# Four accumulator banks a group, the chained bank seeded by ScalarE, in a float32 decoder-layer kernel

## The chip, the cores and the metric

The kernel runs on one core of a Trainium2 chip. The metric is the device time of one execution in microseconds (us). The engines are TensorE (PE in the profile, its weight loads PEld), VectorE (DVE), ScalarE (ACT), GpSimd (POOL) and SyncE (SP, which issues most of the loads). Each has its own instruction queue, worked off in order.

## The reference, cut to what matters

One decoder layer on 256 tokens of width 2048, all in float32, with some 350 MB of weights by their shapes:

```python
h = rmsnorm(x, g_mix);  proj = h @ w_in            # 2048 -> 15872
x_r, g_r, q, k, v, gate_r, gate_a = split(proj)
y_r = (gelu(g_r) * rg_lru(conv(x_r))) @ w_rnn_out  # 2816 -> 2048
y_a = stick_breaking_attention(norm(q), norm(k), v) @ w_attn_out
x = x + (sigmoid(gate_r) * y_r + sigmoid(gate_a) * y_a) @ w_o
g, u = split(rmsnorm(x, g_ffn) @ w_ffn_gu)         # 2048 -> 2 * 5632
x = x + (silu(g) * u) @ w_ffn_down                 # 5632 -> 2048
x = x + sigmoid(rmsnorm(x, g_ple) @ w_ple_gate) * (p @ w_ple_proj)
```

Nearly all of the work is in these matrix products.

## The kernel before, in words

**Products.** Every float32 operand is split in two rounded halves (`hi` from ScalarE, `lo = x - hi` from VectorE). One product of a 128x128 token tile with a 128x512 block of weights is then three matmuls, `hi*hi`, `hi*lo`, `lo*hi` (`prod`). The splits of weights are the tiles `whi`/`wlo` (plain chunks, from `raw`) and `shi`/`slo` (chunks of the seven-product scheme, from `r`), each 128x1024; a chunk is loaded by one DMA of 512 KB.

**Groups.** `group` computes four output banks, two token tiles by two column blocks of 512 (`cols[0]`, `cols[1]`). A k tile is 128 rows of the weights. For some pairs of k tiles (listed in `CFG`) the 2x2x2 block product is done with seven products in place of eight (Winograd's form of Strassen's scheme); the pairs come in twos, a double pair (`dp`), since a chunk holds 1024 columns. The seven steps are named `11`, `22`, `21` (weight blocks as loaded) and `T1` to `T4` (sums of weight blocks, made in place in the tile `r`: by a DMA that adds, issued by POOL (`pr.add`), where the step is listed in `how`, else by VectorE, `r<-r,r`). All other k tiles are plain: each chunk, one k tile of both column blocks, feeds four products.

**Banks before.** A group takes five of the eight PSUM banks: the outputs `q2`, `q4`, `q3`, `q8`, and `U`, in which `11`, `T1`, `T2`, `T3` are accumulated one after the other. At the stations between, `U` is read: ScalarE copies it after `11` (`ja`), VectorE subtracts after `T1` (`je = ja - U`), ScalarE copies it after `T2` (`jc`) and after `T3` (`jd`), and VectorE adds `je = jd + je`. At the end VectorE joins each of the four output banks with one of these four (`join`, or `onto` where the result is added to the residual `x1`).

**Order.** `build` records every operation with its tiles in program order. `schedule` then plans each engine's order with a table of costs, due times counted back from the PE order, and numbers of slots (`ROOM`: 42 tiles of 4 KB, 22 of 2 KB, 8 banks); PE may take an operation up to `WINDOW` = 60 places ahead. `emit` writes the instructions in the planned order, once, so on the chip every queue follows that order whatever happens.

**Stages**, in PE's order before: `xr` (five groups and a half), `ro`, `gtr`, `v`, `qk` with attention between, `gta`, `ao`, `wo`, then `gu` and `dn` mixed, then `pg` with `pp`.

Of the kernel before, what the change touches and what calls it, by code (L numbers as in the profile page):

```python
# [36 lines left out]
class Tile:  # L37


    def __init__(self, name, kind, cols, dt=F32):  # L40
        self.name, self.kind, self.cols, self.dt = name, kind, cols, dt
        self.log, self.ops, self.real, self.slot, self.n = [], [], None, None, 0
# [45 lines left out]
class Program:  # L88
# [102 lines left out]
    def mms(self, jobs, reads, writes, name=""):  # L191


        jobs = list(jobs)
        d = sum(j[3] for j in jobs)

        def emit(nc):
            for o, l, r, _, start, stop in jobs:
                nc.tensor.matmul(o.ap(), l.ap(), r.ap(), start=start, stop=stop)
        return self.op("PE", d, 0.2, emit, reads, writes, name=name)  # L200

    def prod(self, ps, x, w, name=""):
# [5 lines left out]
        def emit(nc, start, stop, again):  # L208
            kw = {"skip_group_check": True} if again else {}
            nc.tensor.matmul(ps.ap(), x[0].ap(), w[0].ap(), start=start, stop=False, **kw)  # L210
            nc.tensor.matmul(ps.ap(), x[0].ap(), w[1].ap(), start=False, stop=False, **kw)  # L211
            nc.tensor.matmul(ps.ap(), x[1].ap(), w[0].ap(), start=False, stop=stop, **kw)  # L212
# [3 lines left out]
    def turns(self, ps, srcs, ident, name=""):  # L216


        def emit(nc):
            for n, s in enumerate(srcs):  # L220
                nc.tensor.transpose(ps[n * P:n * P + P].ap(), s.ap(), ident.ap())  # L221
        return self.op("PE", 0.109 * len(srcs), 0.25, emit, [*srcs, ident], [ps[:P * len(srcs)]], name=name)
# [15 lines left out]
LOAD_US, ADD_US, DMA_LEAD, DMA_TAIL, SPARE, LATE = 1.575 / 512, 2.96 / 512, 1.3, 1.2, 5.0, 2.0  # L238
# [6 lines left out]
def deadlines(prog, boost=None):  # L245
# [5 lines left out]
    for o in reversed(prog.ops):  # L251
# [3 lines left out]
        fin = o.at + (40.0 if o.cap is None else o.cap)  # L255
# [11 lines left out]
def schedule(prog, room, window, boost=None):  # L267
# [15 lines left out]
    free = {k: [(0.0, i, None) for i in range(n)] for k, n in room.items()}  # L283
    pes = [o for o in prog.ops if o.eng == "PE"]
# [13 lines left out]
    def can(o):  # L298
# [4 lines left out]
        for k, ts in want.items():  # L303
            m = max((t.need, t.n) for t in ts)
            i = bisect.bisect_left(wait[k], m)
            if len(free[k]) <= i:
                return False
# [7 lines left out]
    while left or events:  # L315
        moved = True
        while moved:
            moved = False
            for e in ready:
# [11 lines left out]
                else:  # L331
                    for i, (k, _, o) in enumerate(ready[e]):
                        if best is not None and k > best + 3.0:
                            break
                        if o.early is not None and now < o.due - o.early:
# [19 lines left out]
                for t in o.tiles:  # L355
                    if t.kind in room and t.slot is None:
                        if o.eng == "SP":
                            i = max(range(len(free[t.kind])), key=lambda i: free[t.kind][i][:2])
                        else:
                            i = 0  # L360
                        _, t.slot, o.why = free[t.kind].pop(i)
# [23 lines left out]
                moved = True  # L385
        if not events:
            if left:
                for e in ready:
                    print(e, [(round(k, 1), o.name, can(o)) for k, _, o in ready[e][:5]])
                print({k: len(v) for k, v in free.items()},  # L390
                      {k: [(t.name, round(t.need)) for _, _, t in v[:6]] for k, v in wait.items()})
                raise RuntimeError(f"no room at {now}")
            break
        now = events[0][0]
        while events and events[0][0] <= now + 1e-9:
# [7 lines left out]
            for t in o.tiles:  # L403
                t.left -= 1
                if t.left == 0 and t.kind in room:
                    bisect.insort(free[t.kind], (now, t.slot, o), key=lambda x: x[:2])
# [36 lines left out]
def emit(prog, order, nc, tc, pools):  # L443
    first, last, opened = {}, {}, {}
    again, shut = set(), set()
    for o in order:
        for r in o.reads:
            if r.t.kind == "P":
                for k in [k for k in opened if k[0] is r.t and overlap(k[1], k[2], r.a, r.b)]:
                    last[opened.pop(k).n] = True  # L450
                    shut.add(k)
        for r in o.acc:
            k = (r.t, r.a, r.b)
            if k not in first:
                first[k] = o
            if k in shut:
                again.add(o.n)
# [5 lines left out]
    for o in order:  # L463
        for t in o.tiles:
            if t.real is None and t.kind in pools:
                pool = pools[t.kind]
                names[t.name] = names.get(t.name, 0) + 1
                tag = f"{t.kind}{t.slot}" if t.slot is not None else f"k_{t.name}"
# [5 lines left out]
        if o.acc:  # L474
            r = o.acc[0]
            k = (r.t, r.a, r.b)
            o.emit(nc, first[k] is o, o.n in last, o.n in again)
# [14 lines left out]
SPREAD = (0.3, 0.5, 0.65, 0.8)  # L492


def order_of(ks, nd, lead=0):


    ks = list(ks)
    if not nd:
        return ks  # L500
    if lead:
        return ks[:lead] + order_of(ks[lead:], nd)
    n = len(ks)
    cuts = [round(n * f) for f in SPREAD]
    p = [ks[i:j] for i, j in zip([0] + cuts, cuts + [n])]
    s = {m: [(m, d) for d in range(nd)] for m in ("11", "22", "T1", "21", "T2", "T3", "T4")}
    h = (nd + 1) // 2
    return (s["11"] + s["22"] + p[0] + s["T1"] + s["21"][:h] + p[1] + s["T2"] + s["21"][h:] + p[2] + s["T3"] + p[3]
            + s["T4"] + p[4])


def build(cfg):
# [31 lines left out]
    for n in ("h", "l"):  # L544
# [5 lines left out]
    warm = tile("warm", "P")  # L550
    pr.mms([(warm.all, ones_r.all, w1t[0].all, 0.4, True, True) for _ in range(9)], [ones_r.all, w1t[0].all], [warm.all],
           name="warm")
# [64 lines left out]
    def half_sums(h, name):  # L617
# [5 lines left out]
        tt(s1, a22, a21, ALU.subtract, name="hs")  # L623
        stt(s2, s1, -1.0, a11, ALU.mult, ALU.subtract, name="hs")
# [28 lines left out]
    def group(w, cols, ks, pairs, sums, tokens, how, hooks=None, lead=0):  # L653
# [6 lines left out]
        q2, q4, q3, q8 = (psum("q") for _ in range(4))  # L660
        U = psum("u") if nd else None
        chain = {}
        a = e = c = d = None
# [5 lines left out]
        bank = {"21": q2, "22": q3, "T4": q4}  # L669
        for n, x in enumerate(order):  # L670
# [9 lines left out]
            m, dp = x  # L680
            if m in ("11", "22", "21"):
                r, b = {"11": (0, 0), "21": (1, 0), "22": (1, 1)}[m]
                chain[m, dp], chain["b" + m, dp] = raw_of(src(r, b, dp), "r" + m)
# [746 lines left out]
```

## Time and profile before

| | |
|---|---|
| median of the runs shown (3) | 1820.9 us (1820.66 to 1825.76) |
| the profiled execution | 1822.8 us, of which the span from first to last instruction is 1821.1 us |
| PE busy | 1797.6 us, 99% of the span, 8325 matmuls |
| VectorE busy | 1742.5 us, 96%, 2076 instructions |
| ScalarE busy | 1351.9 us, 74%, 1803 instructions |
| POOL busy | 176.3 us, 10%; 200 adding DMAs of 512 KB |
| mean share of the 16 DMA engines | 81%; 420 MB moved |
| mean granted TensorE clock | 0.997 |

A busy PE in this profile is not a PE at its peak: a matmul row lasts 390 ns, yet the next one starts 227 ns later. How much PE loses is read from the distances between starts, not from the busy share.

### The profile page before, as it was taken

The numbers are of one execution on the slowest core, as the hardware profiler recorded it, in microseconds if no ns is written. First come the engines' busy times: TensorE is split into PE (matmuls) and PEld (weight loads), VectorE is DVE, ScalarE is ACT, GpSimd is POOL, SyncE is SP. The second block draws the span as 40 slices with busy tenths as digits, with TensorE's granted clock in tenths as the row PEclk, the third lists the DMA queues.
The fourth block names the chain that finished last, engine by engine and source line by source line (L and its number), as shares of the span: only waits on it lengthen the run. The fifth ranks groups of instructions, "written<-read, shape, count | busy, mean of one in ns | idle before, by whom it ended". The sixth has DMA issues, their size and how long they took to land. (4 is left out here: it accounts for less than half of the span.)

```text
span 1821.1 us, 24029 instructions
## 1 busy us (share of the span) xinstructions
PE 1797.6 (99%) x8325; PEld 1489.7 (82%) x8325; DVE 1742.5 (96%) x2076; ACT 1351.9 (74%) x1803; POOL 176.3 (10%) x209
## 2 busy tenths in 40 slices
PE   9899999999999999999999999999999999999998
PEld 7788888788887888888878888778888788888887
DVE  8999997989999889999899999999999999999998
ACT  7889999856766687889666876666677666767774
POOL 1000000001110110010110011100111001110000
PEclk9999999999999999999999999999999999999999
DMA  9676676689997987768987788788988789889684
GB/s 356 197 213 201 194 211 199 195 245 266 249 251 226 244 238 207 212 188 237 267 251 244 235 229 221 214 227 247 285 238 233 195 246 266 226 236 278 197 233 131
DMA packets 118490, 420.09 MB, mean 231 GB/s; under 512 B 13280, under 2 KB 13664, under 8 KB 118368
## 3 DMA queue, kind: packets, MB, share of 16 engines
q1 hardware_dynamic: 89424, 313.68, 49.0%
q0 software_dynamic: 28800, 104.87, 31.6%
q8 instruction: 65, 1.06, 0.2%
q14 instruction: 57, 0.47, 0.1%
q10 hardware_dynamic: 144, 0.01, 0.0%
HBM read 416.41 MB, written 2.10 MB: 230 GB/s over the span
## 5 line engine op out<-in xcount | busy, mean ns | idle before, releaser
L175 ACT ACTIVATE shi<-r 128x1024 fp32r<-128x1024 f32 x644 | 659.2, 1053 | 233.5 <-DVE r L142 93.2
L142 DVE TENSOR_TENSOR slo<-r,shi 128x1024 fp32r<-128x1024 f32 x644 | 774.4, 1239 | 22.5 <-ACT shi L175 20.8
L142 DVE TENSOR_TENSOR wlo<-raw,whi 128x1024 fp32r<-128x1024 f32 (+2 forms) x310 | 375.5, 1219 | 17.2 <-ACT whi L175 11.1
L175 ACT ACTIVATE whi<-raw 128x1024 fp32r<-128x1024 f32 (+2 forms) x310 | 318.9, 1040 | 49.6 <-PE q L211 15.5
L188 POOL DMA_DIRECT2D r<-in_w_dram x200 | 174.3, 872 | 1605.6 <-DVE slo L142 528.3
L142 DVE TENSOR_TENSOR r<-r,r 128x1024 f32<-128x1024 f32 x168 | 206.6, 1242 | 0.3
L211 PE MATMUL q<-wlo,xg 128*128 128x512 f32 x464 | 182.0, 392 | 2.2 <-DVE wlo L142 1.9
L210 PE MATMUL q<-whi,xg 128*128 128x512 f32 x464 | 182.7, 394 | 0.7 <-ACT whi L175 0.7
L212 PE MATMUL q<-whi,xg 128*128 128x512 f32 x464 | 181.1, 390 | 0.0
L211 PEld LDWEIGHTS q<-wlo,xg 128*128 128x128 f32 x464 | 87.2, 188 | 23.0 <-DVE wlo L142 6.1
L212 PEld LDWEIGHTS q<-whi,xg 128*128 128x128 f32 x464 | 87.1, 188 | 18.5 <-DVE xg L146 0.4
L210 PEld LDWEIGHTS q<-whi,xg 128*128 128x128 f32 x464 | 87.2, 188 | 18.3 <-ACT whi L175 1.1
L211 PE MATMUL u<-slo,hgs 128*128 128x512 f32 x192 | 75.8, 395 | 2.9 <-DVE slo L142 2.9
L211 PE MATMUL u<-slo,xs 128*128 128x512 f32 x198 | 77.9, 394 | 0.6 <-DVE slo L142 0.6
L210 PE MATMUL u<-shi,xs 128*128 128x512 f32 x198 | 78.1, 395 | 0.0
L212 PE MATMUL u<-shi,xs 128*128 128x512 f32 x198 | 77.7, 392 | 0.0
L211 PE MATMUL q<-wlo,hg 128*128 128x512 f32 x192 | 74.9, 390 | 0.8 <-DVE wlo L142 0.8
L210 PE MATMUL u<-shi,hgs 128*128 128x512 f32 x192 | 75.7, 394 | 0.0
L212 PE MATMUL u<-shi,hgs 128*128 128x512 f32 x192 | 75.5, 393 | 0.0
L210 PE MATMUL q<-whi,act 128*128 128x512 f32 x192 | 75.3, 392 | 0.0
L210 PE MATMUL q<-whi,hg 128*128 128x512 f32 x192 | 74.9, 390 | 0.0
L212 PE MATMUL q<-whi,act 128*128 128x512 f32 x192 | 74.8, 390 | 0.0
(443 smaller groups left out, 4108.0 us busy)
## 6 DMA issues: line engine op xcount, KB each, us to landing
raw<-in_w_dram SPq DMA_DIRECT2D x288, 512.0 KB, 5.2
r<-in_w_dram SPq DMA_DIRECT2D x276, 512.0 KB, 5.3
r<-in_w_dram POOLq DMA_DIRECT2D x200, 512.0 KB, 7.7
raw<-in_w_dram SPq DMA_DIRECT2D x16, 448.0 KB, 3.3
xq<-in_x_dram SPq DMA_DIRECT2D x8, 256.0 KB, 7.5
x<-in_x_dram SPq DMA_DIRECT2D x8, 256.0 KB, 6.7
xt<-in_xT_dram SPq DMA_DIRECT2D x7, 256.0 KB, 9.7
raw<-in_w_dram SPq DMA_DIRECT2D x4, 320.0 KB, 2.8
```

The lines of the kernel that those rows point to most:

```text
L142: return self.vec(n, lambda nc: nc.vector.tensor_tensor(o.ap(), a.ap(), b.ap(), op), [a, b], [o], name=name, **kw)
L175: nc.scalar.activation(o.ap(), i.ap(), f, **kw)
L188: return self.op("POOL", 0.85, 0.0, lambda nc: nc.gpsimd.dma_start(o.ap(), src(nc), accum_op=ALU.add), [], [o], size=-kb, name=name)
L210: nc.tensor.matmul(ps.ap(), x[0].ap(), w[0].ap(), start=start, stop=False, **kw)
L211: nc.tensor.matmul(ps.ap(), x[0].ap(), w[1].ap(), start=False, stop=False, **kw)
L212: nc.tensor.matmul(ps.ap(), x[1].ap(), w[0].ap(), start=False, stop=stop, **kw)
```

## The change

The diff has 535 lines; this is what it does.

- **Banks.** A group takes four banks. `U` is now the third output. After step `11`, accumulated in `q2` itself, ScalarE copies `q2` into `U`, from bank to bank (`act(U.all, q2.all, AF.Copy)`, a seeded bank). `T1` is accumulated in `q8` and copied out before the rest of `q8` (`jp`); `T2`, `T3`, `T4` go on `U`. VectorE then makes one difference (`jp = jp - jc`) and two joins; `q2` and `U` are read from the banks as they are. The first group alone (`lead`) works with separate banks as before (`early`).
- **Chunks.** A plain chunk holds two k tiles of one column block (`A` or `B`) in place of one k tile of both.
- **Order of steps.** `ORDER` is `11`, half of `22` and `21`, `T1`, half of the `B` chunks, the rest of `22` and `21`, `T2`, the rest of `B`, `T3`, half of the `A` chunks, `T4`, the rest of `A`.
- **Stages.** `gtr` comes before `ro`, with the last steps of the recurrence hung in its first group. Some double pairs are moved between stages, and the lists `how` are longer. Half sums of `x` for the later stages are made later, and with two subtractions where there was a `scalar_tensor_tensor`.
- **Planner.** No operation is started over 1000 us ahead of its due time, 2 KB tiles may take a free 4 KB slot, a seeded tile only takes a bank whose last use wrote all of it by plain matmuls.

Counted in the two programs: matmuls of 512 columns 7345 before and 7339 now, of 256 columns 548 and 548, of 128 columns 432 and 432. VectorE: 1024-wide 1100 and 1091, 512-wide two-tensor 498 and 385, 128-wide 160 and 176. ScalarE: 1024-wide 932 and 935, 512-wide 394 and 443, table loads 55 and 54. POOL's adding DMAs 200 and 216; loads of 512 KB on SP 564 and 566.

```diff
 def order_of(ks, nd, lead=0):
     ks = list(ks)
+    A, B = ([(h, ks[i], ks[i + 1]) for i in range(0, len(ks), 2)] for h in "AB")
...
+def ORDER(s, A, B, nd):
+    h, n, e = (nd + 1) // 2, (len(B) + 1) // 2, len(A) // 2
+    return (s["11"] + s["22"][:h] + s["21"][:h] + s["T1"] + B[:n] + s["22"][h:] + s["21"][h:] + s["T2"] + B[n:] + s["T3"] + A[:e]
+            + s["T4"] + A[e:])
...
-        q2, q4, q3, q8 = (psum("q") for _ in range(4))
-        U = psum("u") if nd else None
+        q2, q3, q8, U = (psum(n) for n in ("q", "q", "q", "u"))
+        early = {x for x in order if x[0] in "AB"} if lead and nd else ()
+        q4 = psum("q") if early else U
+        w8 = psum("q") if early else q8
+        seeds = nd and not early
+        U.seeded = bool(seeds)
...
-        bank = {"21": q2, "22": q3, "T4": q4}
+        bank = {"21": q2, "22": q3, "T1": w8}
+        if seeds:
+            bank["11"] = q2
...
-            if isinstance(x, int):
-                w_ = wslot([(w, x, m) for b in cols for m in b])
-                for b, ps in enumerate((q2, q3)):
-                    for t, p_ in enumerate((ps, q4 if b == 0 else q8)):
-                        pr.prod(p_.all, tok(tokens, x, t), part(w_, b * 512, 512), name="plain")
+            if m in ("A", "B"):
+                b = "AB".index(m)
+                w_ = wslot([(w, k, c) for k in x[1:] for c in cols[b]])
+                for i, k in enumerate(x[1:]):
+                    for t, ps in enumerate(((q2, q4 if x in early else U), (q3, q8))[b]):
+                        pr.prod(ps.all, tok(tokens, k, t), part(w_, i * 512, 512), name="plain")
                 continue
...
-                if left[m] == 0:
-                    if m == "11":
-                        a = tile("ja", "H")
-                        act(a.all, U.all, AF.Copy, name="ja")
-                    elif m == "T1":
-                        e = tile("je", "H")
-                        tt(e.all, a.all, U.all, ALU.subtract, name="je")
-                    elif m == "T2":
-                        c = tile("jc", "H")
-                        act(c.all, U.all, AF.Copy, name="jc")
-                    else:
-                        d = tile("jd", "H")
-                        act(d.all, U.all, AF.Copy, name="jd")
-                        tt(e.all, d.all, e.all, ALU.add, name="je")
+                if left[m] == 0 and seeds and m == "11":
+                    act(U.all, q2.all, AF.Copy, name="ja")
+                elif left[m] == 0:
+                    got[m] = t = tile({"11": "ja", "T1": "jp", "T2": "jc", "T3": "jd"}[m], "H")
+                    act(t.all, ps.all, AF.Copy, name=t.name)
+                    if "T1" in got and "T2" in got and m in ("T1", "T2"):
+                        tt(got["T1"].all, got["T1"].all, got["T2"].all, ALU.subtract, name="jt")
...
-        return [(q2, a, ALU.add), (q4, e, ALU.add), (q3, c, ALU.subtract), (q8, d, ALU.subtract)]
+        return [(q2, None, None), (U, None, None), (q3, got.get("T1"), ALU.add), (q8, got.get("T3"), ALU.subtract)]
...
-    xp = union("xr", "gtr", "v", "qk", "gta")
+    xp = union("xr", "gtr")
...
-LATER = ("T1", "T3", "T4")
-CFG = dict(xr=[[6, 7]] + [X4] * 4, ro=[F4] * 2, gtr=[X6] * 2, v=[X6] * 2, qk=[X4] * 4, gta=[X4] * 2, ao=[F4] * 2,
-           wo=[F4] * 2, gu=[F4] + [F6] * 10, dn=[[F4] * 2, [[8, 9, 10, 11]] * 2, [[16, 17]] * 2], pg=[F4, F6],
-           how=dict(qk=LATER, gta=LATER, ao=LATER), lead=8, att0=4, every=9, at=(0, 4, 10, 16), turn=[4, 5, 6, 7])
+TWO, LATER, SOON, ALL = [("T1", "T3"), ("T1", "T3", "T4"), ("T1", "T2", "T3"), ("T1", "T2", "T3", "T4")]
+CFG = dict(xr=[[6, 7]] * 2 + [X4] * 3, ro=[F4] * 2, gtr=[X4] * 2, v=[X6] * 2, qk=[X4, X6, X4, X4], gta=[X4] * 2,
+           ao=[F4] * 2, wo=[F4, F6], gu=[F4] + [F6] * 10, dn=[[F4] * 2, [[8, 9, 10, 11]] * 2, [[16, 17, 18, 19]] * 2],
+           pg=[F4, F6],
+           how=dict(xr=[(), LATER, TWO, TWO, ALL], gtr=[LATER, ("T3",)], qk=[SOON, TWO, TWO, TWO], gta=[ALL, LATER],
+                    ro=[SOON, ALL], ao=[TWO, SOON], gu=[TWO] * 7 + [LATER, TWO, TWO, LATER], pg=[SOON, LATER]),
+           lead=8, order=("g1", "r0", "r1"), att0=4, every=9, at=(0, 4, 10, 16), turn=[4, 5, 6, 7])
...
-ROOM = {"L": 42, "H": 22, "P": 8}
+ROOM = {"L": 42, "H": 21, "P": 8}
```

Three places in the planned order. The numbers behind the names tell one buffer from another; `act` and `as` are token tiles and their half sums in the `dn` stage.

**PE in a `dn` group.** Before, `U` is taken up again by `T1`; the last matmul of `11` in `u_13258` stands 45 rows ahead of the first `u` row here:

```order
L212 MATMUL q_13283<-whi_13279,act_12986 128x512
L210 MATMUL q_13327<-whi_13279,act_12986 128x512
L211 MATMUL q_13327<-wlo_13312,act_12986 128x512
L212 MATMUL q_13327<-whi_13279,act_12986 128x512
L210 MATMUL u_13258<-shi_13314,as_12522 128x512 [waits Activation_49]
L211 MATMUL u_13258<-slo_13331,as_12522 128x512 [waits DVE_49]
L212 MATMUL u_13258<-shi_13314,as_12522 128x512
```

Now, the end of `11` in `q_11091` (the third row is its last), one product of `22` in another bank, and `21` in `q_11091` again:

```order
L211 MATMUL q_11091<-shi_10962,act_11032 128x512 [waits Activation_49]
L211 MATMUL q_11091<-slo_10989,act_11032 128x512
L211 MATMUL q_11091<-shi_10962,act_11032 128x512 [waits DVE_49]
L211 MATMUL q_11114<-shi_11025,as_11038 128x512 [waits Activation_49]
L211 MATMUL q_11114<-slo_11064,as_11038 128x512 [waits DVE_49]
L211 MATMUL q_11114<-shi_11025,as_11038 128x512 [waits DVE_49]
L211 MATMUL q_11114<-shi_11025,as_11057 128x512 [waits Activation_49]
L211 MATMUL q_11114<-slo_11064,as_11057 128x512
L211 MATMUL q_11114<-shi_11025,as_11057 128x512 [waits DVE_49]
L211 MATMUL q_11091<-shi_11050,act_11003 128x512 [waits Activation_49]
L211 MATMUL q_11091<-slo_11089,act_11003 128x512 [waits DVE_49]
```

The row that writes `q_11091` again waits for ScalarE's copy of that bank into `U`, and has six matmuls between in place of 44.

**VectorE at the end of a `gu` group.** Before, with the four joins:

```order
L142 TENSOR_TENSOR je_12710<-jd_12848,je_12710 128x512
L142 TENSOR_TENSOR slo_12900<-r_70_12796,shi_12857 128x1024
L142 TENSOR_TENSOR ja_12581<-q_12633,ja_12581 128x512
L142 TENSOR_TENSOR je_12710<-q_12639,je_12710 128x512
L142 TENSOR_TENSOR jc_12767<-q_12576,jc_12767 128x512
L142 TENSOR_TENSOR jd_12848<-q_12649,jd_12848 128x512
```

Now, with two joins and the difference:

```order
L143 TENSOR_TENSOR slo_12058<-r_65_11944,shi_12030 128x1024
L143 TENSOR_TENSOR jp_11900<-jp_11900,jc_11982 128x512
L143 TENSOR_TENSOR jd_12051<-q_11862,jd_12051 128x512
L143 TENSOR_TENSOR jp_11900<-q_11817,jp_11900 128x512
L143 TENSOR_TENSOR slo_12079<-r_63_11963,shi_12037 128x1024
L143 TENSOR_TENSOR slo_12089<-r_64_11980,shi_12053 128x1024
```

Of six 512-wide operations on VectorE in each group (the subtraction after `T1` stands further ahead) three are left.

**ScalarE at the start.** Before, the gained tokens `xg` come ahead of the first weights:

```order
L175 ACT_TABLE_LOAD
L175 ACTIVATE xg_146<-xt_75,gm_69 128x256
L175 ACTIVATE whi_149<-raw_77 128x1024
L175 ACTIVATE shi_153<-r_1_81 128x1024
L175 ACTIVATE whi_165<-raw_83 128x1024
L175 ACTIVATE xg_146<-xt_75,gm_69 128x256
```

Now the first weights come first, on ScalarE and in SP's queue of loads:

```order
L176 ACT_TABLE_LOAD
L176 ACTIVATE whi_157<-raw_75 128x1024
L176 ACTIVATE xg_159<-xt_77,gm_69 128x256
L176 ACTIVATE whi_163<-raw_81 128x1024
L176 ACTIVATE xg_159<-xt_77,gm_69 128x256
L176 ACTIVATE whi_177<-raw_86 128x1024
```

The 512 KB of `raw_75` are now waited for ahead of the 128 KB of `xt`, and the first matmul still needs both.

More of the change, by code (lines that the diff above doesn't have):

```diff
@@ L254, in deadlines @@
             continue
-        fin = o.at + (40.0 if o.cap is None else o.cap)
+        fin = o.at + o.cap if o.cap is not None else 1e9 if o.succ else o.at + 40.0
         if o.cap is None and any(r.t.kind == "P" for r in o.reads):
@@ L306, in can @@
             if len(free[k]) <= i:
+                if k != "H" or len(free["L"]) <= len(want.get("L", ())) + bisect.bisect_left(wait["L"], (m[0] + 15.0, 0)):
+                    return False
+            if k == "P" and any(t.seeded for t in ts) and not any(whole[s] for _, s, _ in free["P"]):
                 return False
@@ L334, in schedule @@
                             break
-                        if o.early is not None and now < o.due - o.early:
+                        if now < o.due - (HORIZON if o.early is None else o.early):
                             continue
@@ L385, in schedule @@
                 moved = True
+        if not events and left:
+            nxt = [o.due - (HORIZON if o.early is None else o.early) for e in ready if e != "PE" for _, _, o in ready[e]]
+            nxt = [t for t in nxt if t > now]
+            if nxt:
+                count += 1
+                heapq.heappush(events, (min(nxt), count, None))
         if not events:
@@ L391, in schedule @@
                       {k: [(t.name, round(t.need)) for _, _, t in v[:6]] for k, v in wait.items()})
+                live = {}
+                for t in prog.tiles:
+                    if t.kind == "L" and t.slot is not None and t.left:
+                        live[t.name] = live.get(t.name, 0) + 1
+                print(live)
                 raise RuntimeError(f"no room at {now}")
@@ L450, in emit @@
                     last[opened.pop(k).n] = True
-                    shut.add(k)
         for r in o.acc:
             k = (r.t, r.a, r.b)
[L454 to L457, printed above, removed]
+            if r.t not in first:
+                first[r.t] = None if r.t.seeded else o
             opened[k] = o
@@ L690, in group @@
             elif m in ("T1", "T3"):
-                if True:
-                    if ("r12", dp) not in chain:
-                        t = chain["r12", dp] = tile("r12", "L")
-                        pr.load(t.all, chain["b12", dp], 512, name="r12")
-                    tt(raw.all, raw.all, chain["r12", dp].all, ALU.add, name="sum")
+                if ("r12", dp) not in chain:
+                    t = chain["r12", dp] = tile("r12", "L")
+                    pr.load(t.all, chain["b12", dp], 512, name="r12")
+                tt(raw.all, raw.all, chain["r12", dp].all, ALU.add, name="sum")
             elif m in ("T2", "T4"):
```

152 lines of the change are left out of this document (81 added, 71 removed).

## The prediction

> **What bounds the kernel now.** First the page's busy times and a table of windows, to see which engine is full where:
>
> ```profile
> PE 1797.6 (99%) x8325; PEld 1489.7 (82%) x8325; DVE 1742.5 (96%) x2076; ACT 1351.9 (74%) x1803; POOL 176.3 (10%) x209
> ...
> 0.00:100.00 100.00, 91.48 (x391) 73.07 (x392) 92.39 (x153) 79.88 (x116) 9.18 (x17) 0.97 0.83 275
> 240.00:340.00 100.00, 99.40 (x546) 85.94 (x546) 89.46 (x118) 95.08 (x133) 3.49 (x4) 1.00 0.65 194
> 1100.00:1200.00 100.00, 98.99 (x438) 80.09 (x437) 100.00 (x114) 69.46 (x82) 10.48 (x12) 1.00 0.81 226
> 1400.00:1500.00 100.00, 97.07 (x426) 79.01 (x425) 97.41 (x108) 63.11 (x73) 10.48 (x12) 0.98 0.82 225
> 1600.00:1700.00 100.00, 100.00 (x454) 82.82 (x453) 100.00 (x111) 70.05 (x83) 8.75 (x10) 1.00 0.87 257
> ```
>
> PE is full nearly everywhere, VectorE nearly as full, so the question is what PE loses. Its pitch (start to start) is read from the timeline where nothing waits: 512-wide, 256-wide, then four 128-wide transposes merged in the chain of waits:
>
> ```profile
> 1519.73 0.39 PE L210 MATMUL q<-shi,act 128*128 128x512 f32 x1
> ...
> 1525.85 0.39 PE L210 MATMUL q<-whi,act 128*128 128x512 f32 x1
> ...
> 227.13 0.28 PE L846 MATMUL rg<-xcs,whi 128*128 128x256 f32 x1
> ...
> 228.08 0.28 PE L848 MATMUL rg<-xcs,wlo 128*128 128x256 f32 x1
> ...
> 1333.06 0.44 PE gut L221 x4
> ```
>
> Twenty-seven pitches in 6.12 us are 0.2267 us; eight in 0.95 us are 0.119; 0.44 / 4 = 0.11. By the program's counts PE's work is 7345 x 0.2267 + 548 x 0.119 + 432 x 0.11 = 1665 + 65 + 48 = 1778 us. The span has a head and a tail besides:
>
> ```profile
> 1.57 3.63 PE L199 MATMUL warm<-w1h,onesr 128*128 128x512 f32 x9 [1.57 <-DVE one L534]
> ...
> 1815.10 0.39 PE L212 MATMUL pp<-whi,pts 128*128 128x512 f32 x1
> ```
>
> So 1821.1 - 1.6 (head) - 5.6 (after the last matmul) - 1778 leaves **36 us that PE loses between matmuls**. Where: the window 0 to 100 holds 391 matmuls (by the timeline 353 of 512, 30 of 256 and 8 of 128 columns), 84.5 us of work, so 14 us are lost there besides the head; by the same sum 1400 to 1500 loses 5.7, 1100 to 1200 loses 3.0, and all the others together some 13. To whom, by the view of waits and by the two longest stalls in the timeline:
>
> ```profile
> PE q L211 <- DVE slo L142: 7.5, 7, 3.1
> PE u L211 <- DVE slo L142: 4.1, 5, 2.1
> PE q L211 <- DVE wlo L142: 3.3, 6, 0.8
> ```
>
> ```profile
> 73.50 0.39 PE L210 MATMUL q<-shi,xg 128*128 128x512 f32 x1
> 77.00 0.79 PE L211 MATMUL q<-slo,xg 128*128 128x512 f32 x1 [3.12 <-DVE slo L142]
> 77.60 0.63 PE L212 MATMUL q<-shi,xg 128*128 128x512 f32 x1
> 78.02 0.63 PE L210 MATMUL q<-shi,xg 128*128 128x512 f32 x1
> ...
> 70.45 1.65 DVE L146 SCALAR_TENSOR_TENSOR xc<-xrt,prm,xc 128x255 f32<-128x255 f32 x4
> 72.62 3.20 DVE L146 SCALAR_TENSOR_TENSOR xc<-xrt,prm,xc 128x253 f32<-128x253 f32 x8
> 75.73 2.35 DVE L142 TENSOR_TENSOR slo<-r,shi 128x1024 fp32r<-128x1024 f32 x2
> ...
> 1433.60 0.50 PE L211 MATMUL u<-slo,hgs 128*128 128x512 f32 x1 [2.08 <-DVE slo L142]
> ```
>
> The pattern is always the second matmul of a product: `hi` is there, `lo` still stands in VectorE's queue, behind work that PE does not need at that moment (here the convolutions, `xc`). VectorE itself does not pause. After a long stall the pitch is 0.43 us for a while (77.60 to 78.02), so a stall of 3.1 us costs some 3 more.
>
> **What the change does to each engine.** Pitches of VectorE and ScalarE, from merged rows where nothing waits (merged length less one duration, over the count less one):
>
> ```profile
> 1532.14 3.49 DVE L142 TENSOR_TENSOR slo<-r,shi 128x1024 fp32r<-128x1024 f32 x3
> 1535.54 2.48 DVE L142 TENSOR_TENSOR x<-q,x 128x512 f32<-128x512 f32 x4
> 1527.08 3.89 ACT L175 ACTIVATE shi<-r 128x1024 fp32r<-128x1024 f32 x4
> ...
> L175 ACT ACTIVATE ja<-u 128x512 f32<-128x512 f32 x40 | 23.6, 590 | 34.1 <-PE u L212 33.9
> ```
>
> That is 1.135 and 0.60 us on VectorE for 1024 and 512 columns, 0.945 us on ScalarE for 1024 and about 0.5 for 512 (0.59 less the overlap).
>
> *PE:* 7339 in place of 7345 matmuls, -1.4 us. Double pairs moved between stages nearly cancel, so PE's work stays the floor.
>
> *VectorE:* 9 fewer 1024-wide (-10 us), 113 fewer 512-wide (-68), 16 more of 128 columns (about 0.2 each, +3): **-75 us, 1743 to about 1668**. None of it is on the path by itself; what it buys is lead over PE.
>
> *ScalarE:* 3 more 1024-wide (+3), 49 more 512-wide (+25), one table load less (1.28): +27 us, 1352 to 1379 of some 1800. Hidden on average, not everywhere. Counting the new order by the PE position of the first matmul that needs each result, and pricing with these pitches, ScalarE has 104 us of work for 100 us of PE's work at 240 to 340 (recurrence and table loads now beside `gtr`; 95 busy before in the row above). The excess of 4 us must be drawn from lead; 0 to 7 us, I take 1.5.
>
> *Stalls of the first 100 us* (14 now): VectorE's work due there falls from 97 to 89 us by the same count. The cold warm-up and the first product stay, some 5 us; of the rest I take 7 back (0 to 9).
>
> *The start:* the first matmul was released by this chain:
>
> ```profile
> 3.09 1.28 ACT L175 ACT_TABLE_LOAD   x1 [3.09 <-DMA xt<-in_xT_dram]
> 4.38 0.51 ACT L175 ACTIVATE xg<-xt,gm 128x256 fp32r<-128x256 f32 x1
> 4.80 1.04 ACT L175 ACTIVATE whi<-raw 128x1024 fp32r<-128x1024 f32 x1
> 6.41 1.06 ACT L175 ACTIVATE shi<-r 128x1024 fp32r<-128x1024 f32 x1 [0.57 <-DMA r<-in_w_dram]
> ```
>
> Now the table load waits for 512 KB in place of 128 KB. Between no delay and the landing of the second 512 KB (6.41 in the last row, 3.3 us after the 3.09), I take +1 us (0 to 3), nearer to no delay since the first 512 KB had landed by 4.80.
>
> *Stalls after 100 us* (22 now): VectorE is over 100 us of work per 100 us of PE in five of the seventeen later stretches before (106 at 1100), in two now (104 at 1100, 107 at 1600; 89.5 at 1400, where 5.7 us went). The stretch at 1600 had 100% VectorE and lost nothing, so single stretches can live on lead. I take 16 back and leave 6 (13 to 21 back).
>
> *Bank handoffs, the new waits.* In the written order 84 matmuls wait for a ScalarE copy of the very bank they continue; for 53 only six matmuls stand between (1.36 us), as in the PE piece above; before there was one. The copy can start when the last matmul has ended, 0.39 - 0.23 = 0.16 us into the gap, takes 0.59, so about 0.6 us are to spare if ScalarE is free, and none if it has just begun a 1024-wide copy. Queued behind the waiting matmul is all of PE. How often ScalarE was free for such copies:
>
> ```profile
> ACT ja L175 <- PE u L212: 33.9, 18, 4.3
> ACT jc L175 <- PE u L212: 23.1, 18, 5.3
> ACT jd L175 <- PE u L212: 12.9, 11, 4.3
> ```
>
> In 47 of 120 cases it stood waiting for PE; else the copy queued, mostly behind one operation. No copy was urgent then; the planner's due times now make them so. From below nothing, from above a 1024-wide copy less the spare at each of the 53, 53 x 0.35 = 19 us; nearer to the low end, since the due time pulls the copies ahead: +4.
>
> The Trainium skill has a rule against such handoffs ("TensorE: Matmul & The Clock Gate", section "A second HAM failure mode: psum-queue depth-cycling"): where PE idles briefly and often between bursts that cycle through the banks, its clock swings between half and full. By its clock-gate section ("What's actually happening") half rate follows an idle window of about 3.4 us; the 0.43 us pitch after the 3.12 us stall fits, while a wait of 0.59 us was not followed by it (pitch 0.24):
>
> ```profile
> 20.11 0.50 PE L211 MATMUL q<-slo,xs 128*128 128x512 f32 x1 [0.59 <-DVE slo L142]
> 20.44 0.40 PE L212 MATMUL q<-shi,xs 128*128 128x512 f32 x1
> 20.68 0.39 PE L210 MATMUL q<-whi,xg 128*128 128x512 f32 x1
> ```
>
> By the rule the sum would be that of the last rival below; by these rows nothing is added.
>
> *DMA:* 16 more adding DMAs and two more loads. Their price:
>
> ```profile
> q1 hardware_dynamic: 89424, 313.68, 49.0%
> q0 software_dynamic: 28800, 104.87, 31.6%
> ```
>
> 0.316 x 1821 / 200 = 2.9 us of all engines for an add, about 1.5 for a load: +49 us on some 1470, so 81% becomes 84%. Waits of POOL are off the path. Hidden behind PE, 0 (0 to +5 where adds and loads crowd, 1300 to 1600). The tail keeps its eight VectorE operations: 0.
>
> **Sum** against the profiled span: -1.4 + 1 - 7 - 16 + 4 + 1.5 = -17.9, so 1803 us. The profiled execution took 1822.8, 1.7 more than its span, while the median is 1820.9; with the same difference to the median, **1803 us**.
>
> **Rivals.**
>
> 1. *PE's floor is reached.* VectorE's lead ends all waits after 100 us (-22), the first stretch gives 9, the handoffs cost nothing: -1.4 + 1 - 9 - 22 = -31, 1790 us. For it: seven of the seventeen later stretches already lose 0.2 us or less. Against: each has to keep its lead with 42 slots shared by all. Chance 0.27.
>
> 2. *The gain is eaten by new crowding.* ScalarE at 240 costs its whole excess (4), the handoffs 8, and VectorE's two full stretches, 4 and 7 us over, keep half of the old stalls alive (-11.5 in place of -23): -1.4 + 1 - 11.5 + 4 + 8 = 0, 1821. Chance 0.11.
>
> 3. *Slower through the handoffs.* If each of the 53 waits for a whole 1024-wide copy beyond its spare (0.95 us each), 50 us come in place of 4: 1849. The time passes 1826.4 once the handoffs cost 27 us in place of 4, a mean of 0.52 us for each. For it: 73 of 120 copies queued. Against: the planner dates them. Chance 0.08.
>
> 4. *The clock falls at handoffs.* A fall costs some 16 matmuls x 0.2 = 3.2 us (as after 77.60). One in each of the 17 groups whose seed has the short gap: 54 us, 1857. Against: the trace shows such a fall only after 2 us or more of idling. The rule of the Trainium skill named above ("TensorE: Matmul & The Clock Gate", "A second HAM failure mode") speaks for it. Chance 0.02.
>
> **How the numbers follow.** My forecast (1795 to 1815) has 0.52. What a measurement can tell from no change is about 0.3%, 5.5 us, so faster means below 1815.4. Faster: 0.52 + 0.27 = 0.79; same 0.11 (rival 2); slower 0.10 (rivals 3 and 4). The range runs from just under the floor of rival 1 almost to rival 2, 1787 to 1819; outside lie rivals 3 and 4, most of rival 2 and a little below the floor.
>
> **What would show it.** VectorE's busy time near 1668 and ScalarE's near 1379; 512-wide pitch unchanged at 0.2267; PE's lost time down from 36 to about 17 us, of which 6 in the first 100; waits of PE for `slo` and `wlo` far below 15 us in all; new rows with PE waiting for ScalarE's `u` or `jp`, 4 us in sum. I am wrong if PE waits for ScalarE by over 10 us, if ScalarE's stretch at 240 to 340 or VectorE's at 1600 shows a wait that did not exist, or if the pitch itself changes with ScalarE writing to PSUM.

## The result, and the profile after

The changed kernel takes 1802.65 us (median of 4 runs, 1800.65 to 1803.76) against 1820.78 us of the kernel before beside it (1820.58 to 1825.76). The ratio is 0.9893, 95% interval 0.9874 to 0.9912. The forecast was 1803, range 1787 to 1819. Two executions of one kernel differ by up to some 5 us here, so the 18 us are clear of that. The profiled execution took 1800.65 us, its span is 1798.9 us.

The page's busy times and DMA queues (packets, MB, share of 16 engines), and the windows shown before (stretch, its length, busy time of PE, PEld, DVE, ACT and POOL with counts, granted clock, DMA share, GB/s), for the changed kernel:

```profile
PE 1789.5 (99%) x8319; PEld 1486.9 (83%) x8319; DVE 1670.9 (93%) x1970; ACT 1375.6 (76%) x1854; POOL 190.3 (11%) x225
...
q1 hardware_dynamic: 89712, 314.73, 49.7%
q0 software_dynamic: 31104, 113.26, 34.4%
```

```profile
0.00:100.00 100.00, 97.92 (x436) 80.24 (x437) 92.59 (x148) 86.03 (x127) 7.47 (x15) 1.00 0.89 298
240.00:340.00 100.00, 99.14 (x524) 84.04 (x523) 86.41 (x112) 95.20 (x130) 5.23 (x6) 1.00 0.71 210
1100.00:1200.00 100.00, 100.00 (x454) 82.80 (x454) 97.40 (x112) 70.47 (x85) 10.77 (x13) 1.00 0.84 227
1400.00:1500.00 100.00, 100.00 (x448) 82.81 (x447) 91.81 (x98) 66.53 (x78) 11.32 (x13) 1.00 0.83 233
1600.00:1700.00 100.00, 100.00 (x458) 82.81 (x457) 98.25 (x121) 80.26 (x108) 13.93 (x16) 1.00 0.94 256
```

Read the matmul counts: 436 in the first 100 us in place of 391, 454 for 438 at 1100, 448 for 426 at 1400. VectorE has nearly the busy time that was forecast (1668), ScalarE too (1379), the DMA share is 84%. The clock stands at 1.00 in each of these windows.

The timeline of PE: the first product, then two rows near the end with nine pitches between them, 1786.26 to 1788.30, so 0.2267 us as before:

```profile
6.01 0.80 PE L211 MATMUL q<-whi,xg 128*128 128x512 f32 x1 [0.28 <-ACT xg L176]
6.88 0.50 PE L211 MATMUL q<-wlo,xg 128*128 128x512 f32 x1
...
1786.26 0.39 PE L211 MATMUL u<-whi,h 128*128 128x512 f32 x1
...
1788.30 0.39 PE L211 MATMUL pp<-whi,pts 128*128 128x512 f32 x1
```

What PE and its weight loads wait for (us in total, times, longest):

```profile
PE u L211 <- ACT jd L176: 1.0, 2, 0.6
...
PE q L211 <- DVE slo L143: 0.2, 1, 0.2
PE q L211 <- DVE wlo L143: 0.2, 1, 0.2
PE q L211 <- ACT u L176: 0.2, 1, 0.2
```

```profile
PEld u L211 <- ACT jd L176: 4.4, 8, 1.0
...
PEld q L211 <- ACT jp L176: 1.0, 3, 0.4
...
PEld q L211 <- ACT u L176: 0.8, 2, 0.4
```

PE's waits for `slo` and `wlo`, 15 us before, are 0.4 us. The largest new one is for `jd`, the copy of `U` after `T3`, and not for the seed `u`.

**A ledger for all runs.** From the first product to the last matmul, I sum each distance between two starts beyond the pitches of the prediction (0.2267, 0.119, 0.11 us). "lo" are the distances ahead of a matmul that reads `slo` or `wlo`, "hi" ahead of `shi` or `whi` (there the splits, the copies and the bank handoffs are waited for), "rest" other matmuls and all excess under 25 ns. "lo" and "hi" are matmuls of 512 columns; one that starts only 0.02 us behind a 128-wide transpose is counted together with the next, which starts about as much later. It is taken from the one profiled execution of each kernel; the prediction's 36 us counts some 2 us ahead of the first product as well.

| us | lost | first 100: lo, hi, rest | later: lo, hi, rest |
|---|---|---|---|
| before | 33.6 | 8.1, 3.2, 0.3 | 12.6, 4.0, 5.3 |
| after | 13.3 | 1.0, 0.4, 0.2 | 2.3, 4.3, 5.1 |

### The profile page after: what moved, and what is told of

It reads as the page before. It is cut to its first block, busy times and chain, and to the rows that moved or that the text cites. A ratio compares the mean times of both kernels' runs of the same rounds, so it can differ in the third digit from the quotient of the medians.

```text
span 1798.9 us, 23932 instructions
## 1 busy us (share of the span) xinstructions
PE 1789.5 (99%) x8319; PEld 1486.9 (83%) x8319; DVE 1670.9 (93%) x1970; ACT 1375.6 (76%) x1854; POOL 190.3 (11%) x225
## 4 chain that ended last, share of the span: by engine, by line
PE 85%; ACT 8%; DVE 4%; issue 2%; DMA 1%; SPq 0%; DVEq 0%; ACTq 0%; POOLq 0%
PE q L211 54%; PE u L211 27%; ACT shi L176 2%; ACT L176 2%; ACT whi L176 2%; DVE slo L143 1%; PE rg L876 1%; DVE wlo L143 1%; ACT rr L176 1%; PE z L200 1%; PE o L200 1%; DMA raw<-in_w_dram 1%; PE gut L220 1%; DVE r L143 1%; DMA r<-in_w_dram 0%
## 5 line engine op out<-in xcount | busy, mean ns | idle before, releaser
L143 DVE TENSOR_TENSOR wlo<-raw,whi 128x1024 fp32r<-128x1024 f32 (+2 forms) x306 | 365.3, 1210 | 17.9 <-ACT whi L176 13.5
L211 PE MATMUL q<-whi,xg 128*128 128x512 f32 x784 | 267.9, 392 | 0.3 <-ACT xg L176 0.3
L211 PE MATMUL q<-shi,hgs 128*128 128x512 f32 x256 | 87.7, 394 | 0.0
L211 PE MATMUL q<-shi,xs 128*128 128x512 f32 x248 | 86.2, 395 | 0.2 <-DVE rr L143 0.2
L211 PE MATMUL q<-shi,hg 128*128 128x512 f32 x256 | 85.2, 393 | 0.0
L211 PE MATMUL q<-shi,xg 128*128 128x512 f32 x244 | 84.0, 393 | 0.2 <-ACT u L176 0.2
L211 PE MATMUL u<-shi,hgs 128*128 128x512 f32 x256 | 82.4, 389 | 0.0
L211 PE MATMUL u<-shi,xs 128*128 128x512 f32 x248 | 82.3, 390 | 0.0
L211 PE MATMUL q<-whi,act 128*128 128x512 f32 x240 | 81.0, 390 | 0.0
L211 PE MATMUL u<-whi,xg 128*128 128x512 f32 x208 | 79.4, 392 | 0.7 <-ACT jd L176 0.6
L211 PE MATMUL q<-whi,y 128*128 128x512 f32 x168 | 56.6, 389 | 0.0
```

The source lines that it names most:

```text
L143: return self.vec(n, lambda nc: nc.vector.tensor_tensor(o.ap(), a.ap(), b.ap(), op), [a, b], [o], name=name, **kw)
L211: nc.tensor.matmul(ps.ap(), x[i].ap(), w[j].ap(), start=a, stop=b, skip_group_check=True)
```

## The experiments

Each time is the median of 4 or 5 runs; the kernel before took 1820.4 to 1821.3 us beside them. The changed kernel's 1802.65 was not measured beside them, so differences to it under some 3 us are not resolved. Wherever the planner sees an edit it plans all engines anew, and such an order can cost a few us by itself (experiment 6 shows one stall of 2.5 us).

**1. VectorE's load put back.** Three kernels add 122 operations to the changed kernel, one at each difference `jt` and each remaining join, 0.6 us each (in the third, three short ones in place of each):

```diff
+    def extra(o, a):                      # called on every jt, join and onto
+        e = o.emit
+        def emit(nc):
+            nc.vector.tensor_tensor(a.all.ap(), a.all.ap(), a.all.ap(), ALU.max)
+            e(nc)
+        o.emit = emit
```

> The changed kernel with 122 more 512-wide VectorE operations (max of a tile with itself), one ahead of each difference and of each join that is left, three a group, put in behind the planner's back: every engine keeps its order, VectorE gets back the 73 us (122 x 0.60) that the bank scheme took away. Theory A (VectorE's lead decides): VectorE busy near 1744 us, PE waits for slo and wlo as before, 1815 to 1828 us. Theory B (the new stage order, moved pairs and longer lists of adds decide, the joins were beside the path): at most 1806.

Measured 1848.6 us (ratio 1.0156, 1.0143 to 1.017), VectorE 1748.9. The direction is A's, the size far above its range. Its order did not allow for the work, so the next one lets the planner know of it:

```diff
         o.emit = emit
+        o.dur *= 2
```

> As the first experiment with 122 extra 512-wide VectorE operations ahead of the difference and the joins (VectorE back to about 1748 us), but now the planner knows their time, so that order and due times allow for them. Theory A, VectorE's lead over PE is what the change bought: part of the stalls for slo and wlo come back even in a plan that knows of the load, 1808 to 1824, with PE's waits for wlo and slo over 8 us. Rival B, the load itself does not matter and the first experiment lost its time through a plan that did not know of it: 1806 or less.

Measured 1833.8 us (1.0074, 1.0062 to 1.0087): 31 more than the changed kernel, and again above A's range. A had the loss come back as waits for `slo` and `wlo`, over 8 us; PE's rows for these two add up to 3.4 us in this run, those for ScalarE's copies to 12.1. But here the work delays the joins, and so the freeing of banks. The third puts it behind them, on a tile that nobody waits for:

```diff
+            e(nc)
+            for _ in range(3):
+                nc.vector.tensor_tensor(later.all.ap(), later.all.ap(), later.all.ap(), ALU.max)
...
+        o.dur += 0.59
```

> As the planned experiment with extra VectorE work, but the extra work (three 128-wide operations on a small tile that nobody reads, about 0.6 us) stands behind the difference and the joins, so that each bank is read and freed as early as in the changed kernel; VectorE about 1745 us again. Theory A, VectorE's load itself: its sums then come late, ScalarE's splits wait for the sums and its copies stand behind the splits: 1820 to 1834, as with the work in front. Rival B, it was the place, the joins that came late and freed the banks late: 1812 or less.

Measured 1840.9 us (1.0111, 1.0097 to 1.0125), above A's range too. Rival B as it was put, 1812 or less, is out: most of the loss does not need extra work ahead of the joins. That late joins play no part isn't shown, since a group's second join still comes behind the first one's extra work. VectorE was busy 1758.3 us. The waits of PE and of ScalarE in this run:

```profile
PE u L211 <- ACT jd L176: 5.4, 6, 1.4
PE q L211 <- ACT jp L176: 4.8, 9, 0.8
PE q L211 <- DVE wlo L143: 4.2, 6, 1.1
PE q L211 <- DVE slo L143: 3.1, 4, 1.8
```

```profile
ACT shi L176 <- DMA r<-in_w_dram: 112.1, 64, 6.5
ACT shi L176 <- DVE r L143: 60.9, 56, 2.9
```

The same two rows of ScalarE in the changed kernel:

```profile
ACT shi L176 <- DMA r<-in_w_dram: 68.9, 52, 4.0
ACT shi L176 <- DVE r L143: 30.0, 31, 1.8
```

ScalarE waits 31 us more for VectorE's sums `r` and 43 us more for loads. ScalarE works in order, so what stands behind such a `shi` is late too, the copies `jd` and `jp` among them, and with them the matmuls that write those banks again. One such place in this run, ScalarE and PE:

```profile
794.86 1.06 ACT L176 ACTIVATE shi<-r 128x1024 fp32r<-128x1024 f32 x1 [1.67 <-DMA r<-in_w_dram]
...
798.03 0.58 ACT L176 ACTIVATE jd<-u 128x512 f32<-128x512 f32 x1
...
798.66 0.50 PE L211 MATMUL u<-whi,xg 128*128 128x512 f32 x1 [1.43 <-ACT jd L176]
```

"hi" later than 100 us is 26 us here, 4 us in the changed kernel, "lo" 15 and 2.3. Of the "hi" loss, 18 us (3 in the changed kernel) are at matmuls that start within 0.07 us of the end of a copy `u`, `jp` or `jd`. With about the load of the kernel before (1758 against 1743 us) the changed kernel is slower than it by 20 us, and by 13 in the second run (1748 us): it stands less lateness. By the rows above that goes in good part through ScalarE's queue; how much is due to the fewer banks was not separated.

**2. VectorE's load taken from the kernel before.** Here the old banks, pairs and order stay, and only sums of weight blocks are left out:

```diff
                     tt(raw.all, raw.all, chain["r12", dp].all, ALU.add, name="sum")
+                    thin()   # 66 of 168, or all: pr.ops[-1].emit = lambda nc: None
```

> The kernel before, order unchanged, with 66 of VectorE's 168 sums of weight blocks left out, evenly spread (that part of the computation is missing): VectorE 1743 - 66 x 1.135 = 1668 us, the load of the changed kernel, with the old banks, chunks, pairs and order. Theory A, VectorE's load is the cause of the stalls: 1800 to 1810, PE's waits for slo and wlo below 6 us. Rival B, banks, order and pairs are needed as well: 1813 or more.

Measured 1811.1 us (0.9948, 0.9934 to 0.9961), between the two. VectorE was busy 1677.5 us. By the ledger the loss after 100 us falls from 21.9 to 11.9 us, the changed kernel's value (11.8), though made up otherwise: "lo" 5.5 and "hi" 2.3 here, 2.3 and 4.3 there. The first 100 us still lose 10.5, in the timeline of this run at the same place as before. By itself that says little, since only two of the six sums in the first 100 us are among the 66:

```profile
73.78 0.39 PE L210 MATMUL q<-shi,xg 128*128 128x512 f32 x1
76.97 0.79 PE L211 MATMUL q<-slo,xg 128*128 128x512 f32 x1 [2.81 <-DVE slo L142]
...
72.59 3.20 DVE L146 SCALAR_TENSOR_TENSOR xc<-xrt,prm,xc 128x253 f32<-128x253 f32 x8
75.71 2.34 DVE L142 TENSOR_TENSOR slo<-r,shi 128x1024 fp32r<-128x1024 f32 x2
```

> The kernel before, order unchanged, with all 168 VectorE sums left out (VectorE about 1550 us). Theory A: nothing waits for VectorE but at the start and at the convolutions in the first 100 us: 1793 to 1803. Rival B: stalls are fixed by the order (the convolutions ahead of slo at 73 us, the 2 us stall at 1434 us) and stay, 1808 or more.

Measured 1805.7 us (0.9918, 0.9905 to 0.9932), again between the two: 10.6 us still lost in the first 100, now without any of the six sums there (VectorE busy 87.1 us of the 100 in place of 92.4), and 8.4 later. Of the two stalls that B named, the one at 77 us stays (2.4 us lost), the one at 1434 us is gone (0.6 us lost at 1400 to 1500 in place of 5.7). So A holds after 100 us and B in the first 100: there it is the order on VectorE (convolutions ahead of a `slo` that PE needs) and not the load.

**3. VectorE's load taken from the changed kernel.**

```diff
                 tt(raw.all, raw.all, other.all, ALU.add, name="sum")
+                pr.ops[-1].emit = lambda nc: None      # at both places, 156 sums
```

> The changed kernel without the 156 VectorE sums of weight blocks (the seven-product chunks use the blocks as loaded; that part of the computation is left out), in the same planned order: VectorE's load falls by 156 x 1.135 = 177 us. If VectorE's queue is what PE still waits for (theory A), PE's lost time falls from some 17 to 8 to 11 us: 1791 to 1797. If the rest comes from loads, ScalarE or bank handoffs: 1799 to 1804.

Measured 1802.5 us (0.9899, 0.9886 to 0.9913), VectorE 1509.9: 161 us less load bring nothing. What PE waited for:

```profile
PE q L211 <- ACT jp L176: 1.8, 3, 0.9
...
PE q L211 <- ACT u L176: 1.4, 1, 1.4
```

So VectorE's load no longer costs the changed kernel anything. The largest waits that are left are for ScalarE's copies; not all of the 15.2 us still lost is put down to a wait by these rows.

**4. The tables.** The whole new table `CFG` (pairs and lists `how`) in the kernel before, then the old lists and the old pairs, each alone, in the changed kernel:

```diff
-CFG = dict(xr=[[6, 7]] + [X4] * 4, ...      # before
+CFG = dict(xr=[[6, 7]] * 2 + [X4] * 3, ...  # the new table whole
```

> The kernel before (five banks, old order of steps, old chunks, old planner) with the new table of pairs and adding DMAs alone. VectorE's load stays near 1737 us (9 fewer 1024-wide operations, 4 more 512-wide), POOL issues 216 adds. Theory A: 1812 to 1824 us. Theory B: 1800 to 1807.

Measured 1830.8 us (1.0058, 1.0044 to 1.0072): slower, which neither theory had. The loss after 100 us is 39 us in place of 22, though in the first 100 it falls from 11.7 to 4.6.

```diff
-           how=dict(xr=[(), LATER, TWO, TWO, ALL], gtr=[LATER, ("T3",)], ...
+           how=dict(qk=LATER, gta=LATER, ao=LATER),
```

> The changed kernel with the old lists of adding DMAs (203 in place of 216; 13 more sums on VectorE, +15 us of its load) and all else new. Theory A: VectorE near 1686 us, still well under PE, 1802 to 1809 us. Theory B: at least 1810.

Measured 1806.7 us (0.9923, 0.9911 to 0.9936), as A had it: 203 adding DMAs in place of 216 and VectorE at 1685.8 cost 4 us, little more than what can be resolved.

```diff
-CFG = dict(xr=[[6, 7]] * 2 + [X4] * 3, ro=[F4] * 2, gtr=[X4] * 2, v=[X6] * 2, qk=[X4, X6, X4, X4], ...
+CFG = dict(xr=[[6, 7]] + [X4] * 4, ro=[F4] * 2, gtr=[X6] * 2, v=[X6] * 2, qk=[X4] * 4, ...
```

> The changed kernel with the double pairs in the stages where they were before (xr, gtr, v, qk, wo, dn as in the old table), the new lists of adding DMAs kept. Theory A, the moved pairs keep ScalarE and VectorE within reach in the gating stages: 1806 to 1815, with more lost between matmuls at 100 to 500 us. Rival B, banks and lists alone bring the gain, and the moved pairs are worth their six matmuls only: 1802 to 1805.

Measured 1814.7 us (0.9968, 0.9956 to 0.9981), A's upper end. Lost: 5.1 us in the first 100 (some 1.8 of them because PE ran at a pitch of 0.43 us from 7.8 to 10.7 us, which was so in this run and the one before it alone), and 11.0 at 300 to 400, where the changed kernel loses 1.4. One such place in this run, PE and ScalarE:

```profile
333.75 0.39 PE L211 MATMUL u<-shi,xs 128*128 128x512 f32 x1
335.36 0.50 PE L211 MATMUL u<-whi,xg 128*128 128x512 f32 x1 [1.22 <-ACT jd L176]
...
332.90 1.28 ACT L176 ACT_TABLE_LOAD   x1
334.19 0.63 ACT L176 ACTIVATE rr<-rr 128x512 f32<-128x512 f32 x1
334.73 0.58 ACT L176 ACTIVATE jd<-u 128x512 f32<-128x512 f32 x1
```

The table alone, pairs and lists, costs 10 us in the kernel before; the change with the old pairs gains 6, and the whole change 18: the table pays only together with the rest of the change. Why it costs in the old scheme was not tested. The rest, which is the banks, chunks, order of steps, order of stages and planner, was only ever run as one, so no run says what the banks bring apart from VectorE's load.

**5. How much spare the handoffs have.** Each seed copied twice in a row:

```diff
-                    act(U.all, q2.all, AF.Copy, name="ja")
+                    o2 = act(U.all, q2.all, AF.Copy, name="ja")
+                    o2.emit = (lambda f: lambda nc: (f(nc), f(nc)))(o2.emit)
```

> The changed kernel with each of the 39 copies of the bank of 11 into U issued twice in a row by ScalarE (about 0.5 us more at each seed, 20 us more of ScalarE in all; the planned order is the same). Theory A, the handoff has spare: half of the copies ended within 0.62 us of the last matmul, so 1.12 us stays inside the six matmuls (1.36 us); only the late tenth (0.92 us and more) becomes a wait: 2 to 6 us more than the changed kernel's 1802.6, so 1803 to 1809, with PE's waits for ScalarE's u up from about 1 to 3 to 7 us. Rival B, the handoffs are at their limit already: 39 x 0.5 us, 1815 or more.

Measured 1811.8 us (0.9951, 0.9939 to 0.9964), 9 us more, 0.23 for each seed: between the two. The weight loads' waits in this run:

```profile
PEld q L211 <- ACT u L176: 10.5, 20, 1.1
PEld q L211 <- ACT jp L176: 4.5, 8, 0.9
```

My count left out the 0.16 us by which the last matmul ends after the gap has begun. With it: 0.16, the usual 0.62 to the copy's end and 0.58 for the second copy are 1.36 us, just the six matmuls; any queue on ScalarE then shows (20 seeds have a matmul right behind their end, 2 in the changed kernel). So the prediction's spare, "about 0.6 us", is what there is.

**6. More matmuls ahead of the handoff after `T3`.**

```diff
-                for i, k in enumerate(x[1:]):
-                    for t, ps in enumerate(((q2, q4 if x in early else U), (q3, q8))[b]):
+                for t, ps in enumerate(((q2, q4 if x in early else U), (q3, q8))[b]):
+                    for i, k in enumerate(x[1:]):
```

> The changed kernel with the four products of a plain chunk ordered bank by bank (both k tiles into q2, then both into U; so also for q3 and q8) in place of k tile by k tile. After the copies of T3 and T1 the first matmul that writes the copied bank again then has six matmuls ahead of it in place of three. Theory A, the handoff after T3 is the largest part of what PE still loses (2.3 us at matmuls whi into u, behind the copy jd): those become less than 1 us and the time 1799 to 1802. Rival B, the late copies are late by ScalarE's queue and not by the gap: 1802 to 1805 and as many waits as before.

Measured 1804.9 us (0.9916, 0.9903 to 0.993), not faster: 8 losses of 2.5 us in all ahead of `whi` matmuls into `u`, 7 of 2.3 us in the changed kernel, and one new stall of 2.5 us (at 663 us) from an order that came out differently. But the edit did less than was expected of it. In the changed kernel's trace, 27 of the 40 copies `jd` already have six 512-wide matmuls between the last one into `U` and the next, nine have nine and three have three (the first group has none); the edit only brings these three to six. So this run hardly tests theory A. That the late copies are late by ScalarE's queue (B) is read from the rows: six of the seven that PE waits for have the gap of six. The two longest stalls of the changed kernel after its start, PE and ScalarE at each:

```profile
326.27 0.39 PE L211 MATMUL u<-shi,xs 128*128 128x512 f32 x1
...
328.37 0.50 PE L211 MATMUL u<-whi,xg 128*128 128x512 f32 x1 [0.58 <-ACT jd L176]
...
325.63 1.28 ACT L176 ACT_TABLE_LOAD   x1
326.93 0.91 ACT L176 ACTIVATE ra<-rr,cA 128x256 f32<-128x256 f32 x2
327.74 0.57 ACT L176 ACTIVATE jd<-u 128x512 f32<-128x512 f32 x1
```

```profile
1216.45 0.39 PE L211 MATMUL u<-shi,as 128*128 128x512 f32 x1
...
1218.64 0.50 PE L211 MATMUL u<-whi,act 128*128 128x512 f32 x1 [0.45 <-ACT jd L176]
...
1216.10 2.01 ACT L176 ACTIVATE shi<-r 128x1024 fp32r<-128x1024 f32 x2 [0.53 <-DVE wlo L143]
1218.02 0.57 ACT L176 ACTIVATE jd<-u 128x512 f32<-128x512 f32 x1
```

`U` was complete at 326.66 and `jd` began at 327.74, behind a table load and two activations of the recurrence; the second time, at 1216.84 and 1218.02, it stood behind two splits, the first of which had waited 0.53 us for VectorE's `wlo`.

**7. One more double pair.** VectorE has room, so PE's own work might be cut further:

```diff
-CFG = dict(xr=[[6, 7]] * 2 + [X4] * 3, ...  how=dict(xr=[(), LATER, TWO, TWO, ALL], ...
+CFG = dict(xr=[[6, 7]] * 2 + [X4] * 2 + [X6], ...  how=dict(xr=[(), LATER, TWO, TWO, LATER], ...
```

> The changed kernel with one more double pair in the last group of xr (six matmuls fewer, 1.4 us) and its T2 sum back on VectorE. Theory A, PE's own work is what is left to save, and VectorE has room for it: 1.4 us less than the changed kernel, 1799.5 to 1802. Rival B, the added chunks meet ScalarE where it is full (100 to 300 us) and give as much back: 1802 to 1807.

Measured 1803.2 us (0.9902, 0.9889 to 0.9916): not told apart from the changed kernel, and in B's range. The ledger shows 18.3 us lost in place of 13.3, so the six matmuls were given back, but not where B had it: 100 to 300 us lose 3.5 in place of 4.0. The new losses are spread (1.1 us more in the first 100, 1.2 at 800 to 900, 1.1 at 1500 to 1600, 1.4 at 1700 to 1800), and all engines were planned anew, so the cause stays open.

## Why the prediction was right, step by step

The two profiled spans differ by 22.2 us, the medians by 18.1; the profiled executions lie on opposite sides of the medians, so the terms below are some 4 us larger in sum than the medians bear. The predicted sum was -17.9.

- *PE:* -1.4 by the count, at an unchanged pitch. *Tail:* the last matmul starts 5.4 us ahead of the end, 6.0 before, -0.6, where 0 was forecast.
- *The start:* predicted +1 (0 to 3), measured 0: the first product's first two matmuls start at 6.01 and 6.88 us, 5.89 and 7.16 before. The table load, which the forecast had wait for the 512 KB, now starts at 1.24 us and waits for no load; the first split starts at 4.51 us, at 4.80 before. What was waited for was `xg`, which now stands behind that split on ScalarE, 0.28 us.
- *First 100 us:* predicted -7 (0 to 9), measured -10.2 (11.7 to 1.5), outside its range. This step was mis-sized and in part mis-reasoned: it was worked out from VectorE's load, which fell from 97 to 89 us by the count. But the kernel before without any of VectorE's sums still loses 10.6 us there, while the new table alone, with the old banks, took the loss to 4.6. It was the order and the pairs of `xr`: the changed kernel loses 3.1 there with the old lists and 5.1 with the old pairs, and 1.8 of each is the slow pitch at 8 to 11 us, so less that, 1.3 and 3.3 against 1.5.
- *Stalls after 100 us:* predicted 16 of 22 back. "lo" fell by 10.3 and "rest" by 0.2: 10.5, below the 13 of the range. Of the 22 us, 4.2 are excess under 25 ns at each matmul, which stayed (4.3) and which no lead of VectorE can return; the forecast counted them as stalls. That the relief is the cause is shown by the kernel before with 66 sums less: -10.0.
- *Handoffs and ScalarE's full stretch:* predicted +4 and +1.5. "hi" went from 4.0 to 4.3, so +0.3 net. Old waits of that kind went (with VectorE lighter in the kernel before, 4.0 became 2.3) and new ones came: at eleven copies the next matmul starts within 0.07 us of the copy's end, and 3.0 us are lost there, 2.3 behind seven copies `jd`, 0.4 behind two seeds, 0.2 behind two copies `jp`. So the mechanism was right and the size, 3 us in place of 5.5, near. Put the old waits to the relief, and that is 13.2 us, the low end of its range. The copy that is mostly late is `jd` after `T3`, not the seed of the forecast's example, though six of the seven have the very gap of six matmuls that it priced. The longest is at 328 us, in the very stretch where ScalarE was counted to be full. The prediction named a new wait at 240 to 340 us as a sign of being wrong, though its own sum had 1.5 us for that stretch; the wait came, and it is 0.58 us long.
- *The sum:* against it, the stalls after 100 us gave 5.5 us less than forecast, handoffs and ScalarE's stretch cost 5.2 less, the first 100 us gave 3.2 more, start and tail 1.6 more. That is -22.4 for the two profiled spans, 4 more than was forecast; the medians differ by 18.1 because these two executions lie 4 us further apart than the medians. The direction and the main term were right; that the medians meet 1803 to within 1 us is in part luck.
- *DMA, pitch:* the DMA share rose to 84% as forecast, and the pitch is unchanged.

The rivals: (1) the floor of 1790 was not reached, by the ledger because of the 4.3 us and of the waits at ScalarE's copies; the changed kernel without VectorE's sums shows that more lead does not bring it. (2) The crowding at 240 and 1600 did not eat the gain: 1600 to 1700 loses 0.3 us at 98% VectorE. (3) The slower rival is real as a mechanism: with VectorE as busy as before, the changed kernel takes 1841 us, with 26 us lost at "hi" matmuls. What decided against it was VectorE's 72 us. (4) The clock is 1.00 in the windows shown, with 84 handoffs. The rival's price of 16 slow matmuls for a fall was too high: in the kernel before there are 12 pitches of 0.43 us after 77.60 and one of 0.59, 2.8 us in all. The Trainium skill ("TensorE: Matmul & The Clock Gate", "A second HAM failure mode: psum-queue depth-cycling") describes a clock that swings between half and full where PE idles briefly and often between bursts that cycle through the banks; no run here shows that over these handoffs, and the nearest thing to it, a single fall after a cluster of waits, stands in the last section.

## What to carry to other kernels

When, as here, the second operand of a product is always what is late, lighten the engine that makes it and look at its order apart from its load: here the load was worth 10 us after the first 100 us, and the order and the placement of the work 10 us in them. A scheme that needs fewer accumulators by copying between them puts the copying engine's queue on the path, so check what stands ahead of each copy, not only how many matmuls lie between; and price the scheme together with the relief that pays for it: here the new table alone lost 10 us, and the new scheme under the old load 13 to 20. A sum that comes out right can hold two wrong terms, so compare it term by term.

## What the runs showed of the hardware

A copy from bank to bank cost ScalarE no more than one from a bank to a tile (585 against 594 ns below), and a matmul that waits for a copy starts 0.06 us after its end (328.31 to 328.37). The two groups in the changed kernel (busy, mean ns of one, idle before and its releaser):

```profile
L176 ACT ACTIVATE jp<-q 128x512 f32<-128x512 f32 x40 | 23.8, 594 | 23.9 <-PE q L211 23.8
...
L176 ACT ACTIVATE u<-q 128x512 f32<-128x512 f32 x39 | 22.8, 585 | 34.3 <-PE q L211 34.2
```

The clock can fall after less idling than the 2 us that the prediction had taken. In the kernel before the granted clock is 0.50 at 77.6 to 82 us, after the stall at 77 us, and the pitch 0.43 us. Over all fourteen profiles, each of the eight single losses of 2.1 us or more was followed by pitches of 0.43 us, two of the ten between 1.6 and 2.1 us, and, after the first 11 us, none of the shorter ones but one: in the kernel with planned extra VectorE work (experiment 1, the second), three waits of 0.65, 1.16 and 0.67 us came within 3.5 us, and the pitch was 0.43 us for 5 us (granted clock 0.50 at 1212 to 1217 us):

```profile
1207.95 0.73 PE L211 MATMUL q<-shi,act 128*128 128x512 f32 x2 [0.65 <-DVE act L143]
...
1210.08 0.63 PE L211 MATMUL q<-shi,act 128*128 128x512 f32 x1 [1.16 <-DVE act L143]
1211.39 0.80 PE L211 MATMUL q<-shi,act 128*128 128x512 f32 x1 [0.67 <-ACT u L176]
...
1214.96 0.63 PE L211 MATMUL q<-shi,act 128*128 128x512 f32 x1
1215.39 0.63 PE L211 MATMUL q<-shi,as 128*128 128x512 f32 x1
```
